# Expert weights streamed through a mixture-of-experts stage: down products one matrix later, a held first load, a last pass in pairs of rows

## The chip, the cores and the metric

The kernel runs on one core of one Trainium2 chip. The metric is the device time of one execution in microseconds (us), the median of several runs; lower is better. All data is fp32.

## The reference

One encoder block on 2048 tokens of 1024 features: two groups of attention heads, an output projection, a mixture of experts, and a last RMSNorm. The change lies in the last two:

```python
gate = g_w * jax.nn.softmax(top_val, axis=-1)     # top group, then the top 2 of its 8 experts
def run_block(args):                              # xb: rows of tokens sent to expert e
    xb, e = args
    h = jax.nn.silu(xb @ w_gate[e]) * (xb @ w_up[e])
    return h @ w_down[e]
y = jnp.zeros((N, D), x.dtype).at[slot_tok].add(ys * slot_gate[:, None])
...
h = h + hier_moe(rms_norm(h, norm2_gain[l]), ...)
return rms_norm(h, final_gain)
```

There are 64 experts; w_gate and w_up are 1024 x 512 each, w_down is 512 x 1024: 6 MiB of weights per expert, 384 MiB in all.

## The kernel before, in words

Up to about 1676 us the kernel computes attention, the projection and the routing; they are not touched. Then comes the **experts' stage**, to about 2951 us, and **the last pass** (`finish`) to the end.

**Pieces.** Each of an expert's three matrices is loaded from DRAM in two pieces of 1 MiB (`raw`, 128 partitions x 8 KB), 384 pieces in all; `halves_of` lists them in order. All loads (L1370) are issued by SP, in that order, each into one of 9 places (`NAHEAD` 5 + `NB` 4). The first five are issued before the stage ("ahead"). Below, piece 5 is the sixth one, and piece 383 the last. DRAM reads and writes of all queues go through the same 16 DMA engines.

**Split.** For exactness, each piece is split into a high part `wh` (a cast, ACT, L1498) and a low part `wl = raw - wh` (a subtraction, DVE, L1500), with `WN` places each. TensorE (PE) multiplies with both: 24 products of 512 columns for each matrix, `pg` (gate) and `pu` (up) at L1547, `py` (down) at L1553.

**An expert's way.** POOL gathers its 100 rows from `d_xn` into `xg` by an indirect DMA (L1507). PE transposes them (L1520), and ACT and DVE split them into `xT` (L1525, L1527). After the gate products ACT takes silu (L1568), and after the up products DVE multiplies into `hh` (L1571). PE transposes `hh` (L1577), and ACT and DVE split it into `hT` (L1581, L1583). After the down products ACT scales them into `o` (L1590), and POOL adds `o` to rows of `d_h` by an indirect DMA, the "put" (L1595). The last put waits for the seven before it, and the last pass reads `d_h` after the last put.

**What sets the order.** The helper functions of `experts` (`loads`, `weights`, `inputs`, `products`, `silu`, `sums`) are generators that ask a planner (`Plan.run`) for an engine with `ask(engine, us, ..., take=places, urge)`. The planner simulates all engines with these costs, and the order in which it grants the requests becomes the program order of PE, ACT, DVE and POOL. On the chip each engine then runs its instructions in that order and waits at each for what it needs. The loads' order on SP is that of `halves_of` whatever the costs.

**The last pass** loads `d_h` in 8 transfers of 1 MiB (L1625; 4 KB pieces per partition), and for each of 16 blocks of 128 rows takes the sum of squares (ACT, L1632), two small POOL operations (L1633, L1634), the scaling (DVE, L1635) and a store of 512 KB (L1636). A second call of `experts` for overflowing rows exists in the program and is not executed with these inputs.

Of the kernel before, what the change touches and what calls it, by code (L numbers as in the profile page):

```python
# [8 lines left out]
F32 = mybir.dt.float32  # L9
# [3 lines left out]
AF = mybir.ActivationFunctionType  # L13
OP = mybir.AluOpType
AX = mybir.AxisListType

P = 128
T = 2048
NT = T // P
D = 1024  # L20
KD = D // P
EPS = 1e-6
# [6 lines left out]
NG = 8  # L29
NE = 64  # L30
CAP = 100
# [13 lines left out]
NPL = 3  # L45
NAHEAD = 5
NB = 4
WN = 4
PYN = 2
WLAND = 30  # L50
LF = 2.9
# [69 lines left out]
class Plan:  # L121
# [19 lines left out]
    def give(self, token, *names):  # L141
        for n in names:
            self.slots.setdefault(n, []).append(token)
# [34 lines left out]
def ask(eng, dur, *deps, take=(), due=None, urge=0.0):  # L178
    return eng, dur, deps, take, due, urge
# [7 lines left out]
def halves_of(n):  # L187


    seq = [(0, 0, 0), (0, 0, 1)]  # L190
    for e in range(n):
        seq += [(e, 1, 0), (e, 1, 1)] + [(e + 1, 0, 0), (e + 1, 0, 1)] * (e + 1 < n) + [(e, 2, 0), (e, 2, 1)]
    return seq


# [1 line left out]
def hybrid_encoder_kernel(ctx, tc, x, norm1_gain, w_in, gla_up_fwd, gla_up_fwd_bias, gla_up_bwd,  # L197
# [3 lines left out]
    nc = tc.nc  # L201
# [65 lines left out]
    def rms_scale(dst, ss, n):  # L267

        nc.vector.tensor_scalar(dst, ss, 1.0 / n, EPS, op0=OP.mult, op1=OP.add)
        nc.gpsimd.tensor_tensor(dst, dst, mhalf[0:dst.shape[0], :dst.shape[-1]], op=OP.pow)  # L270
# [539 lines left out]
    with ExitStack() as ph:  # L810
# [555 lines left out]
        def load_expert(e, raw, which, half):  # L1366
            w = (w_gate, w_up, w_down)[which]

            v = w[0, e].rearrange("(p k) n -> p (k n)", p=P)
            nc.sync.dma_start(raw, v[:, half * 2048:(half + 1) * 2048])  # L1370

        listed = []
        last_h, raw_pools, ahead, taken = [], [], [], [0]

        def next_raw(load):
            pool = raw_pools[len(raw_pools) > 1 and taken[0] % (NAHEAD + NB) >= NAHEAD]
            taken[0] += 1
            raw = pool.tile([P, 2048], F32, name="raw")
            load(raw)
            return raw  # L1380

        def load_ahead(t):
# [28 lines left out]
    with ExitStack() as ph:  # L1411
# [5 lines left out]
        xgs = [wp.tile([CAP, D], F32, name=f"xg{j}") for j in range(2)]  # L1417
        for t in xgs:
            nc.gpsimd.memset(t, 0.0)

        start = wp.tile([P, NE], F32, name="start")
        bexp = wp.tile([1, OBLK], I32, name="bexp")
# [40 lines left out]
        def experts(blocks, ahead=(), then=None):  # L1463


            plan = Plan({"xg": 2, "xT": 2, "hT": 2, "wh": WN, "wl": WN, "pt": 2, "pg": 1, "pu": 1, "py": PYN,
                         "hh": 2, "o": 2, "visit": NG, "raw": NAHEAD + NB - len(ahead)})
            add, give = plan.add, plan.give
            raws, ws, xTs, hTs, ps, nb = {}, {}, {}, {}, {}, len(blocks)
            puts = {}  # L1470
            data_dep = mybir.DependencyInfo(mybir.DependencyClass.Sync, mybir.DependencyReason.DATA)
            seq = halves_of(nb)
            listed_at = TL if ahead else 0.0, "dma"
# [5 lines left out]
            def loads():  # L1479
                for n, (e, which, half) in enumerate(seq):  # L1480
                    t = (0.0, "dma")
                    if n < len(ahead):
                        raws[n] = ahead[n]
                    else:
                        t = yield ask("dma", 2.91, take=("raw",))
                        raws[n] = next_raw(lambda raw: blocks[e][1](raw, which, half))
                    give((t[0] + 2.0, "dma"), f"raw{n}")

            def weights(n):

                k = 4 if seq[n][1] < 2 else 2
                t = yield ask("act", 1.9, take=(f"raw{n}", "wh"))
                if n + 1 < len(seq):
                    add(weights(n + 1))
                raw = raws.pop(n).rearrange("p (k n) -> p k n", k=k)
                wh = sp.tile([P, k, 2048 // k], F32R, name="wh", bufs=WN)
                wl = sp.tile([P, k, 2048 // k], F32R, name="wl", bufs=WN)
                nc.scalar.copy(wh, raw)  # L1498
                t = yield ask("dve", 2.28, t, take=("wl",))
                nc.vector.tensor_tensor(wl, raw, wh.bitcast(F32), op=OP.subtract)  # L1500
                ws[n] = wh, wl
                give(t, "raw", f"w{n}")

            def inputs(e):
                xg = xgs[e % 2]
                t = yield ask("pool", 1.95, listed_at, take=("xg",), urge=20.0)
                nc.gpsimd.indirect_dma_start(  # L1507
                    out=xg, out_offset=None, in_=d_xn, in_offset=bass.IndirectOffsetOnAxis(ap=column(e, 0), axis=0),
                    bounds_check=T - 1, oob_is_err=False)
                t = yield ask("dma", 1.18, (t[0] + 1.5, "pool"), urge=20.0)  # L1510
                if e + 1 < nb:
                    add(inputs(e + 1))
                tx = t[0] + 1.8, "dma"
                xT = sp.tile([P, 2, KD, CAP], F32R, name="xT")
                xk = xg.rearrange("c (p k) -> c k p", k=KD)
                for b in range(2):
                    t = yield ask("pe", 0.42, tx, take=("pt",) if b else ("pt", "xT"), urge=20.0)
                    pt = pp.tile([P, 4, CAP], F32, name="pt")
                    for k in range(4):
                        nc.tensor.transpose(pt[:, k, :], xk[:, 4 * b + k], ident[0:CAP, 0:CAP])  # L1520
                    if b:
                        give(t, "xg")
                    bs = slice(4 * b, 4 * b + 4)
                    t = yield ask("act", 0.49, t, urge=20.0)
                    nc.scalar.copy(xT[:, 0, bs], pt)  # L1525
                    t = yield ask("dve", 0.57, t, urge=20.0)
                    nc.vector.tensor_tensor(xT[:, 1, bs], pt, xT[:, 0, bs].bitcast(F32), op=OP.subtract)  # L1527
                    give(t, "pt")
                xTs[e] = xT
                give(t, f"xT{e}")  # L1530

# [55 lines left out]
            def sums(e):  # L1587
                t = yield ask("act", 1.25, take=(f"py{e}", "o"), urge=40.0)
                o = sp.tile([CAP, D], F32, name="o")
                nc.scalar.activation(o, ps.pop((e, 2)).rearrange("p a b -> p (a b)"), AF.Identity, scale=column(e, 1))  # L1590
                give(t, "py")
                if e + 1 < nb:
                    add(sums(e + 1))
                t = yield ask("pool", 2.9, t, take=("visit",), urge=40.0)
                put = nc.gpsimd.indirect_dma_start(  # L1595
                    out=d_h, out_offset=bass.IndirectOffsetOnAxis(ap=column(e, 0), axis=0), in_=o, in_offset=None,
                    bounds_check=T - 1, oob_is_err=False, compute_op=OP.add)
                for p in range(max(e - NG + 1, 0), e):
                    if e + 1 < nb:
                        tc.declare_no_dep(put.ins, puts[p].ins, reason="tokens of other groups")  # L1600
                    else:
                        tc.add_manual_dep(put.ins, puts[p].ins.name, data_dep, reason="all rows are done")
                if e >= NG:
                    tc.add_manual_dep(put.ins, puts[e - NG].ins.name, data_dep, reason="the group's expert before")
                puts[e] = put
                t = yield ask("dma", 1.18, (t[0] + 1.5, "pool"), urge=40.0)
                give((t[0] + 2.0, "dma"), "visit", "o")
                if then and e == nb // 2:
                    add(then(plan))
# [12 lines left out]

        def finish():

            hs = [next_raw(lambda raw, i=i: nc.sync.dma_start(  # L1625
                raw.rearrange("p (a d) -> p a d", a=2), d_h[2 * i * P:2 * (i + 1) * P].rearrange("(a p) d -> p a d", p=P)))
                for i in range(NT // 2)]
            for i in range(NT):
                h = hs[i // 2][:, i % 2 * D:(i % 2 + 1) * D]
                ss = sp.tile([P, 1], F32, name="ss", bufs=4)  # L1630
                sq = pp.tile([P, 2, 512], F32, name="py", bufs=PYN)
                nc.scalar.activation(sq.rearrange("p a b -> p (a b)"), h, AF.Square, accum_out=ss)  # L1632
                nc.gpsimd.tensor_scalar(ss, ss, 1.0 / D, EPS, op0=OP.mult, op1=OP.add)  # L1633
                nc.gpsimd.tensor_tensor(ss, ss, mhalf[:, :1], op=OP.pow)  # L1634
                nc.vector.scalar_tensor_tensor(h, h, ss, gf, op0=OP.mult, op1=OP.mult)  # L1635
                nc.sync.dma_start(out2[i * P:(i + 1) * P], h)  # L1636
        finish()

        nblk_v = nc.values_load(nblk, min_val=0, max_val=OBLK)
        with tc.If(nblk_v > 0):  # L1640
# [19 lines left out]
            with tc.For_i(0, nblk_v, 1) as b:  # L1660
# [5 lines left out]
                def load(raw, which, half):  # L1666
                    w = (w_gate, w_up, w_down)[which]
                    v = w[0, bass.ds(e, 1)].rearrange("o (p k) n -> p (o k n)", p=P)
                    nc.sync.dma_start(raw, v[:, half * 2048:(half + 1) * 2048])
# [33 lines left out]
```

## Time and profile before

| | |
|---|---|
| median of 3 runs | 2999.57 us (2995.89 to 3000.0) |
| profiled execution | 2999.41 us |
| span of its instructions | 2997.4 us (2.0 us lie outside the span) |
| mean granted TensorE clock | 0.977 |
| PE busy | 94% of the span |
| DMA moved | 647.0 MB, mean 216 GB/s over the span |

The span runs from the first to the last instruction on the core; a clock of 1.0 stands for TensorE's full speed. PE's 94% is an average over stages; the experts' stage is 42% of the time, and what bounds it has to be read there. All times below are us from the span's start.

### The profile page before, as it was taken

What the parts mean: (1) busy time and instruction counts of PE and PEld (TensorE: products, weight loads), DVE (VectorE), ACT (ScalarE), POOL (GpSimd) and SP (SyncE); (2) the same over time, 40 slices, a digit from 0 to 9 for tenths busy, and PEclk for the clock granted to TensorE, in tenths of its full rate; (3) what the DMA queues carried; (4) which work ended last, traced back from release to release, by engine and by line L of the source; (5) the groups of instructions that cost most, each with busy time, mean ns of one, the idle gap of its engine ahead of it and who ended that gap; (6) DMA issues with size and microseconds to landing.
All of it is one profiled execution on the core that took longest, in us unless ns stands there. A gap on an engine that the chain in (4) does not pass through costs nothing.

```text
span 2997.4 us, 38671 instructions
## 1 busy us (share of the span) xinstructions
PE 2819.4 (94%) x13776; PEld 2096.9 (70%) x13776; DVE 2222.5 (74%) x3214; ACT 1857.9 (62%) x2776; POOL 468.2 (16%) x349
## 2 busy tenths in 40 slices
PE   7999999999999999999999699999999999999992
PEld 6888788887677777777677466666666666666661
DVE  6654788888666766776766688887778878788784
ACT  4433333333676777777776477777777767777773
POOL 3443111111000000000000211111111111112114
PEclk9999999999899999999999799999999999999996
DMA  7874333223522222221221799999999999999996
GB/s 256 293 263 167 140 105 108 76 104 124 195 66 66 68 67 67 66 71 60 75 64 57 284 357 356 356 357 345 347 346 351 342 346 355 347 349 346 342 317 233
DMA packets 177316, 647.00 MB, mean 216 GB/s; under 512 B 39013, under 2 KB 53703, under 8 KB 123549
## 3 DMA queue, kind: packets, MB, share of 16 engines
q1 hardware_dynamic: 138942, 590.92, 55.1%
q0 software_dynamic: 23712, 34.36, 5.2%
q10 hardware_dynamic: 14464, 19.21, 2.0%
q8 instruction: 109, 1.79, 0.3%
q14 instruction: 89, 0.73, 0.1%
HBM read 546.08 MB, written 117.13 MB: 221 GB/s over the span
## 4 chain that ended last, share of the span: by engine, by line
PE 72%; DMA 14%; DVE 5%; ACT 5%; issue 2%; POOL 1%; SPq 0%; ACTq 0%; POOLq 0%; DVEq 0%
PE py L1553 9%; DMA raw<-in_w_up_dram 8%; PE pu L1547 7%; PE pg L1547 7%; PE pm L1007 6%; PE pm L681 4%; PE pa L1356 4%; PE ps L1328 4%; PE pa L1354 4%; PE pa L1355 4%; PE ps L1329 4%; DMA raw<-in_w_down_dram 3%; PE pv L334 3%; PE pqk L334 3%; DVE wl L1500 2%
## 5 line engine op out<-in xcount | busy, mean ns | idle before, releaser
L1500 DVE TENSOR_TENSOR wl<-raw,wh 128x2048 fp32r<-128x2048 f32 x384 | 872.3, 2289 | 242.8 <-ACT wh L1498 242.2
L1498 ACT CAST wh<-raw 128x2048 fp32r<-128x2048 f32 x384 | 726.0, 1903 | 245.9 <-PE py L1553 102.0
L1343 DVE TENSOR_TENSOR p_l<-p,p_h 128x512 fp32r<-128x512 f32 x512 | 344.0, 689 | 200.2 <-ACT p_h L1340 194.1
L1332 ACT ACTIVATE p<-ps 128x512 f32<-128x512 f32 x512 | 296.4, 599 | 150.3 <-PE ps L1329 132.6
L1553 PE MATMUL py<-wh,hT 128*100 128x512 f32 x1024 | 306.5, 412 | 56.2 <-ACT hT L1581 42.5
L683 DVE TENSOR_REDUCE nm<-pm 128x1 f32<-128x1024 f32 x256 | 305.0, 1216 | 46.7 <-PE pm L681 46.6
L1547 PE MATMUL pg<-wh,xT 128*100 128x512 f32 x1024 | 334.7, 397 | 0.0
L1547 PE MATMUL pu<-wh,xT 128*100 128x512 f32 x1024 | 330.5, 393 | 0.0
L1340 ACT CAST p_h<-p 128x512 fp32r<-128x512 f32 x448 | 268.9, 624 | 5.8
L1553 PEld LDWEIGHTS py<-wh,hT 128*100 128x100 f32 x1024 | 163.0, 169 | 143.2 <-ACT hT L1581 52.7
L1547 PEld LDWEIGHTS pg<-wh,xT 128*100 128x100 f32 x1024 | 170.5, 167 | 64.1
L1547 PEld LDWEIGHTS pu<-wh,xT 128*100 128x100 f32 x1024 | 168.0, 164 | 67.5
L1507 POOL DMA_INDIRECT xg<-d_xn,L x64 | 124.9, 1952 | 577.5 <-PE pt L1520 570.2
L1328 PE MATMUL ps<-q,K 128*128 128x512 f32 x512 | 210.6, 411 | 1.2 <-ACT p L1332 0.8
L1354 PE MATMUL pa<-p_h,V 128*66 128x512 f32 x512 | 204.4, 399 | 0.0
L1356 PE MATMUL pa<-p_l,V 128*66 128x512 f32 x512 | 202.7, 396 | 0.9 <-DVE p_l L1343 0.9
L1329 PE MATMUL ps<-q,K 65*128 65x512 f32 x512 | 203.4, 397 | 0.0
L1547 PE MATMUL pg<-wl,xT 128*100 128x512 f32 x512 | 202.0, 395 | 0.0
L1355 PE MATMUL pa<-p_h,V 128*64 128x512 f32 x512 | 201.5, 393 | 0.0
L1547 PE MATMUL pu<-wl,xT 128*100 128x512 f32 x512 | 200.5, 392 | 0.0
L1595 POOL DMA_INDIRECT d_h<-o,L x64 | 102.1, 1595 | 471.6 <-ACT o L1590 471.6
L681 PE MATMUL pm<-K,q 128*128 128x512 f32 x512 | 169.6, 416 | 1.1 <-DVE nm L683 1.1
(416 smaller groups left out, 5098.9 us busy)
## 6 DMA issues: line engine op xcount, KB each, us to landing
raw<-in_w_gate_dram SPq DMA_DIRECT2D x128, 1024.0 KB
raw<-in_w_up_dram SPq DMA_DIRECT2D x128, 1024.0 KB
raw<-in_w_down_dram SPq DMA_DIRECT2D x128, 1024.0 KB
d_uT<-uT SPq DMA_DIRECT2D x16, 1024.0 KB
uT<-d_uT SPq DMA_DIRECT2D x15, 1024.0 KB
x_t<-in_x_dram SPq DMA_DIRECT2D x16, 512.0 KB
wraw<-in_w_in_dram SPq DMA_DIRECT2D x32, 256.0 KB
d_q<-q ACTq DMA_DIRECT2D x16, 512.0 KB
```

The source lines that it names most:

```text
L683: nc.vector.tensor_reduce(nm[:, h, b:b + 1], pm, axis=AX.XY, op=OP.max, negate=True)
L1328: nc.tensor.matmul(ps, lhsT=K1[:, kv, ks], rhs=r1, start=True, stop=False)
L1329: nc.tensor.matmul(ps, lhsT=K2[:, kv, ks], rhs=r2, start=False, stop=True)
L1332: nc.scalar.activation(p, ps, AF.Exp)
L1343: nc.vector.tensor_tensor(p_l, p, p_h.bitcast(F32), op=OP.subtract)
L1354: nc.tensor.matmul(pa, lhsT=hi, rhs=p_h, start=(kt == 0), stop=False)
L1355: nc.tensor.matmul(pa[0:DH], lhsT=V[:, kt, kv, 0:DH], rhs=p_h, start=False, stop=False)
L1356: nc.tensor.matmul(pa, lhsT=hi, rhs=p_l, start=False, stop=(kt == NT - 1))
L1498: nc.scalar.copy(wh, raw)
L1500: nc.vector.tensor_tensor(wl, raw, wh.bitcast(F32), op=OP.subtract)
L1547: nc.tensor.matmul(acc_p, lhsT=xTs[e][:, a, k, :], rhs=w[:, kk, :], start=(k == 0 and a == 0 and w is wh), stop=(k == KD - 1 and a == 1))
L1553: nc.tensor.matmul(acc_p[:, c], lhsT=hTs[e][:, a, k, :], rhs=w[:, kk, c * 512:(c + 1) * 512], start=(k == 0 and a == 0 and w is wh), stop= ...
```

## The change

Four things are changed. (1) `halves_of`: the order of pieces was gate 0; then for each expert e up e, gate e+1, down e. It is now gate e, up e, down e-1, so that a gate and an up matrix stand between an expert's up products and its down products (one matrix, the next gate, stood there before). `WN` goes from 4 to 5. (2) Piece 5 waits until expert 0's gather has landed, and the first subtraction waits until POOL has issued that gather (a 1x1 memset, `issued`, stands behind it on POOL); both of expert 0's transposes are asked for ahead of its splits, with a higher urge. (3) Costs of the planner: a load 2.91 to 2.6, a gather 1.18 to 0.8, a put 1.18 to 1.3. (4) `finish` takes two adjacent rows of tokens to a partition: 8 loads and 8 stores of 1 MiB, 8 KB for each partition, and `rms_scale` for a pair (one DVE and one POOL operation) in place of two POOL operations per block.

```diff
-WN = 4
+WN = 5
...
-    seq = [(0, 0, 0), (0, 0, 1)]
-    for e in range(n):
-        seq += [(e, 1, 0), (e, 1, 1)] + [(e + 1, 0, 0), (e + 1, 0, 1)] * (e + 1 < n) + [(e, 2, 0), (e, 2, 1)]
+    seq = []
+    for e in range(n + 1):
+        seq += [(x, which, half) for x, which in ((e, 0), (e, 1), (e - 1, 2)) for half in range(2) if 0 <= x < n]
...
-        def next_raw(load):
+        def next_raw(load, after=None):
...
+            ld = load(raw)
+            if after is not None:
+                tc.add_manual_dep(ld.ins, after.ins.name, ..., reason="the first rows go before")
...
-                        t = yield ask("dma", 2.91, take=("raw",))
+                        after = ahead and n == len(ahead)
+                        t = yield ask("dma", 2.6, take=("raw", "landed") if after else ("raw",))
...
-                t = yield ask("dve", 2.28, t, take=("wl",))
+                t = yield ask("dve", 2.28, t, take=("wl",) if n else ("wl", "issued"))
...
+                if e == 0:
+                    first.extend((get, nc.gpsimd.memset(issued, 0.0)))
+                    give(t, "issued")
-                t = yield ask("dma", 1.18, (t[0] + 1.5, "pool"), urge=20.0)
+                t = yield ask("dma", 0.8, (t[0] + 1.5, "pool"), urge=20.0)
...
-                t = yield ask("dma", 1.18, (t[0] + 1.5, "pool"), urge=40.0)
+                t = yield ask("dma", 1.3, (t[0] + 1.5, "pool"), urge=40.0)
...
+            pair = lambda a, i: a[2 * i * P:2 * (i + 1) * P].rearrange("(p a) d -> p (a d)", a=2)
+            hs = [next_raw(lambda raw, i=i: nc.sync.dma_start(raw, pair(d_h, i))) for i in range(NT // 2)]
+            for i, h in enumerate(hs):
+                ss = sp.tile([P, 2], F32, name="ss", bufs=4)
+                for a in range(2):
...
+                rms_scale(ss, ss, D)
+                for a in range(2):
+                    ha = h[:, a * D:(a + 1) * D]
+                    nc.vector.scalar_tensor_tensor(ha, ha, ss[:, a:a + 1], gf, op0=OP.mult, op1=OP.mult)
+                nc.sync.dma_start(pair(out2, i), h)
```

Three places show what the planner makes of it. Line numbers move: L1547 becomes L1569, L1553 becomes L1575, L1577 becomes L1599, L1500 becomes L1505, L1527 becomes L1548, L1571 becomes L1593 and L1507 becomes L1514.

**Middle of the stage, PE, before.** The last gate products of one expert, transposes of the next expert's rows and of this expert's `hh`, and the first down products (numbers tell tiles apart):

```order
L1547 MATMUL pg_22468<-wl_22433,xT_22103 100x512
L1547 MATMUL pg_22468<-wh_22432,xT_22103 100x512
L1520 MATMUL pt_22504<-cst_sb_99,xg1_18103 128x100 x4
L1577 MATMUL pt_22512<-cst_sb_99,hh_22365 128x100 x4
L1553 MATMUL py_22530<-wh_22446,hT_22517 100x512 x2
```

The same place on PE in the changed kernel:

```order
L1569 MATMUL pu_22382<-wh_22309,xT_21941 100x512
L1540 MATMUL pt_22420<-cst_sb_99,xg1_18103 128x100 x4
L1575 MATMUL py_22430<-wh_22351,hT_22308 100x512 x2
L1575 MATMUL py_22430<-wl_22352,hT_22308 100x512 x2
L1575 MATMUL py_22430<-wh_22351,hT_22308 100x512 x4
L1575 MATMUL py_22430<-wl_22352,hT_22308 100x512 x2
L1575 MATMUL py_22430<-wh_22351,hT_22308 100x512 x2
L1599 MATMUL pt_22448<-cst_sb_99,hh_22386 128x100 x4
L1575 MATMUL py_22430<-wh_22366,hT_22308 100x512 x2
```

Before, the down products follow right behind the transposes that make their own `hT` (22517). Now they use the `hT` of the expert before (22308), and the transposes of `hh` (22386), for a later `hT`, stand between the two halves of the down products.

**Start of the stage, POOL and DVE, changed kernel.** POOL's first gathers, and DVE from the last step of the routing list (L1306) on:

```order
L1514 DMA xg0_18102<-d_xn_90,L_67 100x1024
L1518 MEMSET issued_18106 1x1
L1514 DMA xg1_18103<-d_xn_90,L_67 100x1024
```

```order
L1306 TENSOR_TENSOR L_67<-pt_18078,L_67 100x64
L1505 TENSOR_TENSOR wl_18119<-raw_17808,wh_18118 128x2048
L1505 TENSOR_TENSOR wl_18126<-raw_17837,wh_18125 128x2048
L1548 TENSOR_TENSOR xT_18121<-pt_18134,xT_18121 128x400
L1548 TENSOR_TENSOR xT_18121<-pt_18141,xT_18121 128x400
L1505 TENSOR_TENSOR wl_18131<-raw_17888,wh_18130 128x2048
```

Before, POOL's row of the memset was not there, and DVE had three subtractions in a row behind L1306; now two, the first of which waits for POOL's memset. On SP the load of piece 5 has one more wait, for the gather's landing, and all later loads stand behind it.

**End of the stage, PE, changed kernel.** The last down products of the last but one expert (`py_27338`) and of the last (`py_27372`):

```order
L1575 MATMUL py_27338<-wh_27277,hT_27246 100x512 x2
L1599 MATMUL pt_27352<-cst_sb_99,hh_27306 128x100 x4
L1575 MATMUL py_27338<-wh_27289,hT_27246 100x512 x2
...
L1575 MATMUL py_27338<-wh_27289,hT_27246 100x512 x2
L1575 MATMUL py_27372<-wh_27312,hT_27357 100x512 x2
```

DVE's end in the changed kernel:

```order
L1505 TENSOR_TENSOR wl_27278<-raw_27125,wh_27277 128x2048
L1505 TENSOR_TENSOR wl_27290<-raw_27147,wh_27289 128x2048
L1505 TENSOR_TENSOR wl_27313<-raw_27170,wh_27312 128x2048
L1505 TENSOR_TENSOR wl_27326<-raw_27201,wh_27325 128x2048
L1593 TENSOR_TENSOR hh_27306<-pu_27302,hh_27306 100x512
L1605 TENSOR_TENSOR hT_27357<-pt_27352,hT_27357 128x400
```

Both kernels have the last expert's multiply (`hh`) behind the last piece's subtraction on DVE. Before, the last expert's up products stood behind the down products of the last but one; now its transposes stand in the middle of those, and between the two last experts' down products there is nothing else.

## Rows read from the trace of the kernel before

**Rows 1.** Page, busy time by engine and costliest groups (busy us, mean ns | idle before)

```profile
PE 2819.4 (94%) x13776; PEld 2096.9 (70%) x13776; DVE 2222.5 (74%) x3214; ACT 1857.9 (62%) x2776; POOL 468.2 (16%) x349
...
L1500 DVE TENSOR_TENSOR wl<-raw,wh 128x2048 fp32r<-128x2048 f32 x384 | 872.3, 2289 | 242.8 <-ACT wh L1498 242.2
L1498 ACT CAST wh<-raw 128x2048 fp32r<-128x2048 f32 x384 | 726.0, 1903 | 245.9 <-PE py L1553 102.0
```

**Rows 2.** Windows mid-stage: length, busy of PE, PEld, DVE, ACT, POOL, clock, DMA share, GB/s

```profile
1800.00:1900.00 100.00, 97.09 (x448) 70.06 (x447) 81.96 (x53) 74.81 (x59) 18.23 (x11) 1.00 1.02 356
2500.00:2600.00 100.00, 93.87 (x430) 67.43 (x429) 79.82 (x51) 71.50 (x57) 17.15 (x10) 1.00 1.01 350
```

**Rows 3.** Chain of waits around one expert's down products: start, us, what

```profile
1980.53 0.60 ACT hh L1568
...
1981.51 0.42 ACT hT L1581
1981.97 5.90 PE py L1553 x24
```

**Rows 4.** Windows of the casts (L1498) alone, cast to cast: length, ACT, clock, share, GB/s

```profile
2020.20:2887.30 867.10, 499.71 (x264) 0.99 1.00 347
```

**Rows 5.** Windows at the start of the stage, columns as in Rows 2

```profile
1668.00:1680.00 12.00, 2.39 (x9) 1.76 (x8) 9.38 (x33) 7.99 (x8) 4.97 (x5) 0.59 0.93 342
1680.00:1687.00 7.00, 0.00 (x0) 0.00 (x0) 2.92 (x2) 0.00 (x0) 5.05 (x2) 0.50 1.02 428
1687.00:1694.00 7.00, 0.31 (x2) 0.31 (x3) 0.00 (x0) 0.00 (x0) 0.00 (x0) 0.50 0.76 238
1694.00:1700.00 6.00, 4.83 (x21) 3.64 (x20) 3.81 (x5) 1.97 (x4) 2.44 (x2) 0.50 0.11 21
1700.00:1709.00 9.00, 9.00 (x39) 6.37 (x38) 3.79 (x4) 6.60 (x5) 0.47 (x1) 0.95 0.70 208
1709.00:1720.00 11.00, 10.80 (x54) 7.88 (x53) 10.12 (x9) 8.19 (x8) 1.23 (x1) 1.00 0.94 346
```

**Rows 6.** Windows at the end of the weights, columns as in Rows 2

```profile
2920.00:2926.00 6.00, 5.38 (x25) 3.77 (x24) 5.13 (x4) 4.69 (x4) 0.00 (x0) 1.00 0.13 40
2926.00:2930.00 4.00, 4.00 (x19) 2.86 (x18) 3.02 (x2) 2.00 (x2) 0.00 (x0) 1.00 0.00 0
```

**Rows 7.** Timeline of POOL, gathers at the start: start, us, what [idle before]

```profile
1677.12 6.86 POOL L1507 DMA_INDIRECT xg<-d_xn,L  x1 [7.03 <-DVE L L1306]
...
1697.18 1.06 POOL L1507 DMA_INDIRECT xg<-d_xn,L  x1 [11.83 <-PE pt L1520]
```

**Rows 8.** Timeline of DVE and of PE over the same stretch

```profile
1676.24 6.68 DVE L1500 TENSOR_TENSOR wl<-raw,wh 128x2048 fp32r<-128x2048 f32 x3
...
1693.69 0.93 PE L1520 MATMUL pt<-cst_sb,xg 100*128 100x100 f32 x4 [17.77 <-DMA xg<-d_xn,L]
```

**Rows 9.** The gathers' line, all 64, us from issue to landing

```profile
DMA to landing us min/median/max: 5.3/11.7/16.5
```

**Rows 10.** Chain of waits, the end of the stage

```profile
2935.44 0.70 DVE hh L1571
...
2936.18 0.74 PE pt L1577 x4
2936.94 0.50 ACT hT L1581
...
2937.49 5.78 PE py L1553 x24
2943.29 1.12 ACT o L1590
...
2944.70 6.63 DMA d_h<-o,L
```

**Rows 11.** Timeline of POOL, the last put but one

```profile
2931.32 1.58 POOL L1595 DMA_INDIRECT d_h<-o,L  x1 [16.39 <-ACT o L1590]
```

**Rows 12.** Windows of the last pass, columns as in Rows 2

```profile
2954.00:2992.00 38.00, 0.00 (x0) 0.00 (x0) 20.55 (x16) 18.05 (x32) 28.18 (x32) 0.50 1.03 415
```

More of the change, by code (lines that the diff above doesn't have):

```diff
@@ L1369, in load_expert @@
             v = w[0, e].rearrange("(p k) n -> p (k n)", p=P)
-            nc.sync.dma_start(raw, v[:, half * 2048:(half + 1) * 2048])
+            return nc.sync.dma_start(raw, v[:, half * 2048:(half + 1) * 2048])
         listed = []
         last_h, raw_pools, ahead, taken = [], [], [], [0]
-        def next_raw(load):
+        def next_raw(load, after=None):
             pool = raw_pools[len(raw_pools) > 1 and taken[0] % (NAHEAD + NB) >= NAHEAD]
@@ L1378, in next_raw @@
             raw = pool.tile([P, 2048], F32, name="raw")
-            load(raw)
+            ld = load(raw)
+            if after is not None:
+                tc.add_manual_dep(ld.ins, after.ins.name, mybir.DependencyInfo(
+                    mybir.DependencyClass.Sync, mybir.DependencyReason.DATA), reason="the first rows go before")
             return raw
@@ L1419, in hybrid_encoder_kernel @@
             nc.gpsimd.memset(t, 0.0)
+        issued = wp.tile([1, 1], F32, name="issued")
         start = wp.tile([P, NE], F32, name="start")
@@ L1466, in experts @@
             plan = Plan({"xg": 2, "xT": 2, "hT": 2, "wh": WN, "wl": WN, "pt": 2, "pg": 1, "pu": 1, "py": PYN,
-                         "hh": 2, "o": 2, "visit": NG, "raw": NAHEAD + NB - len(ahead)})
+                         "hh": 2, "o": 2, "visit": NG, "raw": NAHEAD + NB - len(ahead), "issued": 0, "landed": 0})
             add, give = plan.add, plan.give
             raws, ws, xTs, hTs, ps, nb = {}, {}, {}, {}, {}, len(blocks)
-            puts = {}
+            puts, first = {}, []
             data_dep = mybir.DependencyInfo(mybir.DependencyClass.Sync, mybir.DependencyReason.DATA)
@@ L1484, in loads @@
                     else:
-                        t = yield ask("dma", 2.91, take=("raw",))
-                        raws[n] = next_raw(lambda raw: blocks[e][1](raw, which, half))
+                        after = ahead and n == len(ahead)
+                        t = yield ask("dma", 2.6, take=("raw", "landed") if after else ("raw",))
+                        raws[n] = next_raw(lambda raw: blocks[e][1](raw, which, half), first[0] if after else None)
                     give((t[0] + 2.0, "dma"), f"raw{n}")
@@ L1498, in weights @@
                 nc.scalar.copy(wh, raw)
-                t = yield ask("dve", 2.28, t, take=("wl",))
-                nc.vector.tensor_tensor(wl, raw, wh.bitcast(F32), op=OP.subtract)
+                t = yield ask("dve", 2.28, t, take=("wl",) if n else ("wl", "issued"))
+                lo = nc.vector.tensor_tensor(wl, raw, wh.bitcast(F32), op=OP.subtract)
+                if n == 0:
+                    tc.add_manual_dep(lo.ins, first[1].ins.name, data_dep, reason="the first rows go before")
                 ws[n] = wh, wl
@@ L1506, in inputs @@
                 t = yield ask("pool", 1.95, listed_at, take=("xg",), urge=20.0)
-                nc.gpsimd.indirect_dma_start(
+                get = nc.gpsimd.indirect_dma_start(
                     out=xg, out_offset=None, in_=d_xn, in_offset=bass.IndirectOffsetOnAxis(ap=column(e, 0), axis=0),
                     bounds_check=T - 1, oob_is_err=False)
-                t = yield ask("dma", 1.18, (t[0] + 1.5, "pool"), urge=20.0)
+                if e == 0:
+                    first.extend((get, nc.gpsimd.memset(issued, 0.0)))
+                    give(t, "issued")
+                t = yield ask("dma", 0.8, (t[0] + 1.5, "pool"), urge=20.0)
                 if e + 1 < nb:
@@ L1513, in inputs @@
                 tx = t[0] + 1.8, "dma"
+                if e == 0:
+                    give(tx, "landed")
                 xT = sp.tile([P, 2, KD, CAP], F32R, name="xT")
                 xk = xg.rearrange("c (p k) -> c k p", k=KD)
[L1516 to L1522, printed above, removed]
-                    bs = slice(4 * b, 4 * b + 4)
[L1524 to L1528, printed above, removed]
+                steps = [("pe", 0), ("act", 0), ("dve", 0), ("pe", 1), ("act", 1), ("dve", 1)]
+                urge, ts, pts = 20.0, {}, {}
+                if e == 0:
+                    steps.sort(key=lambda x: ("pe", "act", "dve").index(x[0]))
+                    urge = 60.0
+                for eng, b in steps:
+                    bs = slice(4 * b, 4 * b + 4)
+                    if eng == "pe":
+                        t = yield ask("pe", 0.42, tx, take=("pt",) if b else ("pt", "xT"), urge=urge)
+                        pts[b] = pp.tile([P, 4, CAP], F32, name="pt")
+                        for k in range(4):
+                            nc.tensor.transpose(pts[b][:, k, :], xk[:, 4 * b + k], ident[0:CAP, 0:CAP])
+                        if b:
+                            give(t, "xg")
+                    elif eng == "act":
+                        t = yield ask("act", 0.49, ts[b], urge=urge)
+                        nc.scalar.copy(xT[:, 0, bs], pts[b])
+                    else:
+                        t = yield ask("dve", 0.57, ts[b], urge=urge)
+                        nc.vector.tensor_tensor(xT[:, 1, bs], pts[b], xT[:, 0, bs].bitcast(F32), op=OP.subtract)
+                        give(t, "pt")
+                    ts[b] = t
                 xTs[e] = xT
@@ L1623, in finish @@
         def finish():
[L1625 to L1636, printed above, removed]
+            pair = lambda a, i: a[2 * i * P:2 * (i + 1) * P].rearrange("(p a) d -> p (a d)", a=2)
[3 more added lines that the diff above has]
+                for a in range(2):
+                    sq = pp.tile([P, 2, 512], F32, name="py", bufs=PYN)
+                    nc.scalar.activation(sq.rearrange("p a b -> p (a b)"), h[:, a * D:(a + 1) * D], AF.Square,
+                                         accum_out=ss[:, a:a + 1])
+                rms_scale(ss, ss, D)
[3 more added lines that the diff above has]
+                nc.sync.dma_start(pair(out2, i), h)
         finish()
```

## The prediction

> **What bounds the kernel now.** I read the page first, then windows of 100 us through the experts' stage, then the chain of waits at its middle and its end, then timelines of the queues where the change cuts. The page shows PE busy for 94% of the span [rows 1], which tempts one to look for PE's idle time. The windows [rows 2] are to be read from their last columns: PE is busy 97 of 100 us in one and 94 in another, but the share of the DMA engines is 1.01 to 1.02 in both, at 356 and 350 GB/s. The chain of waits there runs through PE: silu (0.60 us) and the split of hT (0.42) pass through ACT one after the other, with a split of the next rows between, and 1.44 us after silu began the down products run [rows 3]. This is a stall of PE, but is it what sets the stage's pace?
>
> The casts give the pace. From the start of one at 2020.20 to the start of another at 2887.30 there are 264 of them in 867.1 us, 3.284 us for each, with the DMA share at 1.00 [rows 4]: loads were never out of work. With loads alone on the queues they run at 428 GB/s (from 1680 to 1687, [rows 5]), which is 2.45 us for a piece of 1.0486 MB. So an expert takes 6 x 3.284 = 19.70 us, its six pieces alone would take 14.70, and the 5.0 us between are what one gather and one put cost the loads. At the end of the weights one sees where: from 2920 to 2926 the DMA share is 0.13, two engines of 16, at 40 GB/s, and then nothing [rows 6]. Two engines bring the last pieces long after the other 14 are done. I conclude that the stage is bound by its two slowest DMA engines, with PE close behind: it idles 6.1 us in 100 [rows 2], 1.2 us per expert.
>
> **1. Order of pieces and a fifth place.** The change moves the down products away from the transposes that they wait for. With PE as the bound it would return most of 1.2 us per expert. But pieces, gathers and puts are the same in number and size, so by the DMA reading the pace stays at 3.284 us and PE waits as much for weights as it waited for hT: 0 in the middle of the stage. Bounds: the two windows [rows 2] differ by 1.7% in rate, about 20 us over the some 1,200 us of loading. As much as that could go either way if gathers and puts fall differently among the loads; a gain of 1.2 us x 62 experts = 74 us is the naive extreme.
>
> **2. The start.** The first gather takes POOL 6.86 us, from 1677.12 to 1683.98 [rows 7], while DVE does three subtractions without a gap from 1676.24 to 1682.92 [rows 8]. A gather that meets no such row takes 1.06 us [rows 7]: the first one ends 1.06 us after the subtractions, as if it had only begun then. PE's wait for it ends at 1693.69 [rows 8]. Now the first subtraction waits for the gather, so I take it at 1.06 us, and its landing at the shortest time seen, 5.3 us from issue [rows 9], since no load is on the queues: 1677.1 + 5.3 = 1682.4. What waits behind: on DVE two subtractions and then the splits, some 1 us later than before; on SP all loads from piece 5 on, which go at 1682.5 instead of from 1669 on, with first bytes an assumed 1.2 us later, at 1683.7.
>
> What this costs is a matter of bytes. Before, from 1668 to 1720, the windows [rows 5] add up to 4.10 + 3.00 + 1.67 + 0.13 + 1.87 + 3.81 = 14.57 MB; there was a hole from 1694 to 1709, while the places were full and PE waited for rows. After: 36.3 us x 0.428 = 15.54 MB from 1683.7 on. Off this go three gathers; two of them brought the rate to 238 for 7 us, (428 - 238) x 7 / 2 = 0.67 MB each, so 13.5 MB; and what still moves before 1683.7 (rows of d_xn, the last gain, the first gather) I estimate at 1.3 MB. That makes 14.8, ahead by 0.2 MB or 0.5 us. Counted by share of engines, before stood idle for 12 x 0.07 + 7 x 0.24 + 6 x 0.89 + 9 x 0.30 + 11 x 0.06 = 11.2 us, and after would for 12.6: 1.4 us later. With gathers that cost only their bytes (100 rows of 4 KB, 0.41 MB) it is 0.8 MB more, 2.4 us earlier. I take the middle of the two ends, **-0.5**, with bounds -2.4 and +1.4.
>
> **3. The end.** Let the last piece land at 2926 [rows 6]. Before, one more expert's up products stood behind down products, and the chain ended in hh, transposes, hT and the last down products (0.70, 0.74, 0.50, 5.78 us), PE being done at 2943.27; then o, and the put that landed at 2944.70 + 6.63 = 2951.33 [rows 10], 25.3 us after the piece. After: the last piece is cast (1.90) and subtracted (2.29) [rows 1], and only then comes the last expert's multiply (0.70), for which PE's transposes stand in the middle of the next to last down products: 2926 + 0.1 + 1.90 + 2.29 + 0.70 = 2931.0. Then transposes 0.74, the second half of one down product (5.78 / 2 = 2.9) and the whole last one (5.78): PE ends at 2940.4, 2.9 us earlier. But a new wait comes up: the last put waits for the put before. That was 13.4 us ahead (2931.32 [rows 11] against 2944.70), and is now only a down product ahead: its o begins at 2934.6, it is issued 1.4 us later (as 2943.29 to 2944.70) at 2936.0, and lands 6.63 later at 2942.7. The last put could go at 2940.4 + 1.4 = 2941.8; it goes at about 2942.8 and lands at 2949.4. The end comes **-1.9** us after the last piece, with bounds -2.9 (no such wait) and +3.2 (the put before takes the 11.7 us of a gather among loads [rows 9]).
>
> **4. The last pass.** From 2954 to 2992 the DMA share is 1.03 at 415 GB/s; DVE is busy 21 of these 38 us, ACT 18, POOL 28 [rows 12]. It moves 15.8 MB. Pieces of 8 KB at the loads' 428 GB/s would take 36.85 us, a gain of 1.15. Part of the traffic is now stores, for which 428 is not shown, so I take **-0.9** (bounds -1.15 and 0). Fewer POOL and DVE steps save nothing, since DMA covers them; were that cover gone, the pairs would show as gaps between stores.
>
> The Trainium skill, "DMA: Bandwidth & Descriptors", section "Why small descriptors are slow", gives each packet some 3 cycles of overhead at 32 bytes a cycle. By that, 8 KB instead of 4 KB would save 1.1% of the last pass, an estimate of 0.4 us, and the sum would be 2996.6. The rows' difference in rate, 3%, is larger, and decides.
>
> **5. Planner costs** only change the order, which is the one weighed above: 0.
>
> The sum: -0.5 - 1.9 - 0.9 = -3.3 us, from 2999.41 of the profiled execution (0.2 us under the median): **2996.1**.
>
> **Rivals.**
> - *Nothing gained* (2998 to 3001): the held loads cost their bound of +1.4, and the put before lands 2 us later than alone, so that the end's -1.9 goes: +1.4 + 0 - 0.9 = +0.5, 2999.9. It decides from 8.6 us for that put on; alone on the queues it has no reason for it.
> - *Held for a slow gather (slower)*: if the gather still lands at about 1693.7 [rows 8], because its 6.86 us were not the subtractions', loads go 11.3 us later: -0.5 + 11.3 - 1.9 - 0.9 = +8, 3007. It decides from a landing at about 1689 on. For it speaks that no row shows a gather beside fewer subtractions; against it, the match of 1.06 us.
> - *PE is the bound*: 62 experts x 1.2 = -74, about 2925. Against it speak shares of 1.00 and equal spacing of pieces; for it, only the chain through PE.
> - *The slow engines are relieved*: gathers and puts fall into other gaps and cost 5% less, 0.25 x 61 = -15, near 2981; the rate's differences between windows [rows 2] allow as much.
>
> On the second rival the Trainium skill, "SBUF — State Buffer", is of two minds: its section "Who interferes with whom" says that a DVE operation with both inputs in SBUF holds up a GpSimd one that reads SBUF, but it infers that such a subtraction does not hold back the writing of descriptors. By the inference the gather would stay slow and the time near 3007; the trace agrees with the first (the 1.06 us above).
>
> **How the numbers follow.** The sum holds with 0.57 (its own range 2990 to 2999.5; a third of this below 2993.6), nothing gained 0.11, slow gather 0.08, PE-bound 0.06, relieved engines 0.18. A measurement tells 0.2%, 6.0 us, from no change: faster means under 2993.6, slower over 3005.6. Faster: 0.19 + 0.06 + 0.18 = 0.43; same: 0.38 + 0.11 = 0.49; slower 0.08. The range of 2979 to 3001 leaves out the slow gather, PE-bound, and a third of the relieved case, 0.20.
>
> **What would show it.** Right: the first gather at about 1.1 us on POOL and landing near 1682, no hole in DMA between 1694 and 1709, casts still 3.28 us apart with a DMA share of 1.00 while the down products no longer wait for hT, a last put that waits for the one before, 425 GB/s or more in the last pass. Wrong: a spacing of casts under 3.25 us (engines relieved or PE the bound), or a first gather over 5 us.

## The result and the profile after

The changed kernel takes 2982.57 us (median of 6 runs, 2978.75 to 2986.49) against 2999.26 us for the kernel before (6 runs): ratio 0.9947, 95% interval 0.9933 to 0.9961. It is 16.7 us faster; 3.3 were forecast. The profiled execution took 2981.33 us with a span of 2979.4, 18.0 less than before.

Where these 18.0 us lie follows from when pieces land (the semaphore updates that each load sends, in the trace). Counted from the routing list's end (L1306, 1676.3 us before, 1677.5 after; this 1.2 us lies ahead of everything that the change touches):

| | before | after | difference |
|---|---|---|---|
| list's end to piece 15 landed | 43.8 | 46.9 | +3.1 |
| piece 15 to piece 383 landed | 1206.1 | 1183.0 | -23.1 |
| piece 383 to the first load of d_h | 25.2 | 25.7 | +0.5 |
| that load to the span's end | 46.1 | 46.3 | +0.2 |

So the middle of the stage brought all of the gain and more: 368 pieces at 3.215 us in place of 3.277 us.

The windows at the start, columns as in [rows 2], answer to [rows 5]:

```profile
1668.00:1680.00 12.00, 3.35 (x19) 2.56 (x19) 6.11 (x34) 6.45 (x8) 4.76 (x7) 0.63 0.24 88
1680.00:1687.00 7.00, 1.60 (x8) 1.29 (x8) 5.68 (x5) 2.01 (x3) 3.93 (x2) 0.50 0.54 156
1687.00:1694.00 7.00, 6.55 (x25) 4.91 (x26) 6.75 (x4) 4.34 (x4) 0.58 (x1) 0.67 1.02 343
1694.00:1700.00 6.00, 6.00 (x28) 4.28 (x27) 4.00 (x3) 5.97 (x6) 0.83 (x1) 1.00 1.03 330
1700.00:1709.00 9.00, 9.00 (x47) 6.84 (x46) 6.84 (x6) 5.38 (x6) 0.43 (x1) 1.00 1.02 356
1709.00:1720.00 11.00, 11.00 (x53) 8.10 (x52) 10.88 (x8) 7.27 (x7) 2.87 (x2) 1.00 1.02 343
```

The hole of before (share 0.11 from 1694 to 1700) is gone, but a new one stands from 1668 to 1683, and behind it the rate is 330 to 356 GB/s, not 428. The timelines of POOL (first gather), DVE (first subtractions) and SP (piece 5) show the order that was wanted: gather, then subtractions, then loads:

```profile
1678.32 1.19 POOL L1514 DMA_INDIRECT xg<-d_xn,L  x1 [7.03 <-DVE L L1306]
...
1679.63 4.49 DVE L1505 TENSOR_TENSOR wl<-raw,wh 128x2048 fp32r<-128x2048 f32 x2 [2.10 <-POOL issued L1518]
...
1683.82 0.33 SPq L1370 DMA_DIRECT2D raw<-in_w_gate_dram  x1
```

In the middle, the casts from one start to another, as in [rows 4]; then, from 2000 to 2850 us, waits of PE and ACT before (in each row who waited for what: us in total, times, longest), and the longest waits of DVE, ACT and PE after:

```profile
2021.01:2859.12 838.11, 490.49 (x260) 0.98 0.99 353
```

```profile
PE py L1553 <- ACT hT L1581: 31.4, 42, 2.2
...
ACT wh L1498 <- DMA raw<-in_w_up_dram: 30.6, 33, 2.5
...
ACT wh L1498 <- DMA raw<-in_w_down_dram: 28.1, 30, 2.0
```

```profile
DVE wl L1505 <- ACT wh L1503: 155.3, 154, 2.6
ACT wh L1503 <- DMA raw<-in_w_up_dram: 98.7, 60, 3.4
ACT wh L1503 <- DMA raw<-in_w_gate_dram: 49.0, 36, 2.4
PEld pt L1599 <- DVE hh L1593: 37.5, 14, 3.8
```

260 casts in 838.11 us are 3.224 us for each, where [rows 4] gave 3.284. The down products no longer wait for hT; ACT waits longer for loads instead (148 us in these two rows, 59 before). The DMA share is 0.99, where it was 1.00, but the rate is 353 GB/s and not 347: with their share as full as before, the engines carry the same bytes in less time.

The end, in the chain of waits (start, us, what), answers to [rows 10], and the window of the last pass to [rows 12]:

```profile
2918.64 6.76 DMA d_h<-o,L
...
2926.32 6.72 DMA d_h<-o,L
...
2933.10 4.88 DMA raw<-d_h
```

```profile
2936.00:2974.00 38.00, 0.00 (x0) 0.00 (x0) 20.56 (x24) 17.50 (x32) 5.59 (x8) 0.50 1.01 417
```

The last put waits for the one before it, and only then come the loads of d_h; the last pass runs at 417 GB/s against 415.

### The profile page after: what moved, and what is told of

Same layout as the page of the kernel before. It is cut to its first block, busy times and chain, and to the rows that moved or that the text cites. A ratio compares the mean times of both kernels' runs of the same rounds, so it can differ in the third digit from the quotient of the medians.

```text
span 2979.4 us, 38648 instructions
## 1 busy us (share of the span) xinstructions
PE 2812.6 (94%) x13776; PEld 2101.0 (71%) x13776; DVE 2225.4 (75%) x3222; ACT 1852.0 (62%) x2776; POOL 448.4 (15%) x326
## 4 chain that ended last, share of the span: by engine, by line
PE 59%; DMA 21%; issue 7%; DVE 6%; ACT 5%; POOL 1%; ACTq 0%; SPq 0%; POOLq 0%; DVEq 0%
DMA raw<-in_w_gate_dram 10%; DMA raw<-in_w_up_dram 7%; PE pm L1007 6%; PE pm L681 4%; PE pa L1356 4%; PE ps L1328 4%; PE pa L1354 4%; PE pa L1355 4%; PE py L1575 4%; PE pg L1569 4%; PE ps L1329 4%; PE pv L334 3%; PE pqk L334 3%; DVE wl L1505 2%; ACT wh L1503 2%
## 5 line engine op out<-in xcount | busy, mean ns | idle before, releaser
L1505 DVE TENSOR_TENSOR wl<-raw,wh 128x2048 fp32r<-128x2048 f32 x384 | 873.5, 2289 | 218.2 <-ACT wh L1503 215.6
L1569 PE MATMUL pg<-wh,xT 128*100 128x512 f32 x1024 | 335.4, 398 | 0.0
L1569 PE MATMUL pu<-wh,xT 128*100 128x512 f32 x1024 | 330.7, 394 | 0.0
L1575 PE MATMUL py<-wh,hT 128*100 128x512 f32 x1024 | 320.7, 416 | 0.0
L1514 POOL DMA_INDIRECT xg<-d_xn,L x64 | 109.2, 1707 | 914.6 <-PE pt L1540 904.5
L1569 PEld LDWEIGHTS pu<-wh,xT 128*100 128x100 f32 x1024 | 168.1, 164 | 68.2
L1569 PEld LDWEIGHTS pg<-wh,xT 128*100 128x100 f32 x1024 | 170.7, 167 | 64.6
L1575 PEld LDWEIGHTS py<-wh,hT 128*100 128x100 f32 x1024 | 170.3, 176 | 55.6
L1569 PE MATMUL pg<-wl,xT 128*100 128x512 f32 x512 | 202.0, 395 | 0.0
L1569 PE MATMUL pu<-wl,xT 128*100 128x512 f32 x512 | 200.5, 392 | 0.0
L1575 PE MATMUL py<-wl,hT 128*100 128x512 f32 x512 | 166.3, 407 | 0.0
```

The costliest lines, as they stand in the source:

```text
L1505: lo = nc.vector.tensor_tensor(wl, raw, wh.bitcast(F32), op=OP.subtract)
L1569: nc.tensor.matmul(acc_p, lhsT=xTs[e][:, a, k, :], rhs=w[:, kk, :], start=(k == 0 and a == 0 and w is wh), stop=(k == KD - 1 and a == 1))
L1575: nc.tensor.matmul(acc_p[:, c], lhsT=hTs[e][:, a, k, :], rhs=w[:, kk, c * 512:(c + 1) * 512], start=(k == 0 and a == 0 and w is wh), stop= ...
```

## The experiments

**Two theories for the faster middle.** Look at POOL's timeline before, from 2513 us, and after, from 2515 us:

```profile
2513.53 1.73 POOL L1507 DMA_INDIRECT xg<-d_xn,L  x1 [9.16 <-PE pt L1520]
2521.66 1.59 POOL L1595 DMA_INDIRECT d_h<-o,L  x1 [6.39 <-ACT o L1590]
```

```profile
2515.84 2.12 POOL L1514 DMA_INDIRECT xg<-d_xn,L  x1 [17.55 <-PE pt L1540]
2518.26 3.56 POOL L1617 DMA_INDIRECT d_h<-o,L  x1 [0.30 <-ACT wh L1503]
```

Before, a put started 8.1 us behind a gather. In the new order of pieces the second half of the transposes that free a gather's place stands right behind the end of the down products on PE (2514.86 and 2513.12 us here), and the put starts 2.4 us behind the gather. Theory N: gather and put close together cost the loads less than the same two apart. Theory S: the gain comes from PE's earlier start, the fifth place or the later down products, and the distance is an accident.

**1. Puts apart again, all else as changed** (`a_putlate`). Each put waits for the first half of the up products two experts on.

```diff
+                    if (which, half) == (1, 0) and e >= 2:
+                        late[e - 2] = lastmm[0]
+                        give(t, f"late{e - 2}")
...
+                if held:
+                    tc.add_manual_dep(put.ins, late[e].ins.name, data_dep, reason="put later")
```

> The changed kernel, with each put held back until the first half of the up products two experts on has run, so that it starts some 8 us behind the gather in place of some 2 us; nothing else is changed. Theory N (gather and put issued close together cost the loads less than the same two apart): the spacing of casts goes from 3.245 back to about 3.28 us, the time to about 2994 (+8 to +14 us on the changed kernel's 2982.6), ratio to before about 0.998. Theory S (the faster loads come of PE's earlier start, the fifth place and the later down products, not of the puts): no change, 2982 to 2984, ratio 0.995.

Measured: 3002.1 us, ratio to before 1.0012 (1.0003 to 1.0021); the whole gain is gone, more than the 8 to 14 us expected. POOL shows the distance, 8.9 us:

```profile
2507.41 1.29 POOL L1515 DMA_INDIRECT xg<-d_xn,L  x1 [6.43 <-PE pt L1541]
2516.28 2.60 POOL L1624 DMA_INDIRECT d_h<-o,L  x1 [7.59 <-issue]
```

**2. Puts close by, all else as before** (`b_putlate`): the same edit in the kernel before, with (0, 1), the gate products, in place of (1, 0).

> The kernel before, with each put held back until the gate products two experts on have run, so that it starts within some 2 us of a gather in place of 8 to 10 us behind it; nothing else is changed. Theory N: the spacing of casts goes from 3.282 to about 3.25 us and the time falls by 8 to 14 us, to about 2988, ratio 0.996. Theory S: no change, 2997 to 3001, ratio 1.000.

Measured: 2959.28 us, ratio 0.986 (0.9845 to 0.9875): 39.9 us faster than before with none of the change in it, some three times what Theory N expected, and 23 faster than the changed kernel. The put now starts 2.4 us ahead of the next gather:

```profile
2510.62 2.13 POOL L1602 DMA_INDIRECT d_h<-o,L  x1 [15.35 <-ACT hh L1574]
2513.06 1.10 POOL L1508 DMA_INDIRECT xg<-d_xn,L  x1 [0.30 <-issue]
```

Loads no longer set the pace in this run. Its window from 2000 to 2600 us (columns as in [rows 2]) and waits of ACT and PE from 2000 to 2850 us:

```profile
2000.00:2600.00 600.00, 582.25 (x2679) 419.64 (x2678) 496.74 (x327) 446.06 (x350) 106.30 (x64) 1.00 1.01 361
```

```profile
ACT wh L1499 <- PE py L1556: 62.2, 45, 1.4
...
PE py L1556 <- ACT hT L1587: 25.1, 43, 0.6
```

No cast waits for a load here: ACT waits until PE frees places, and PE, busy for 824.7 of these 850 us, waits for hT alone in nearly all the rest. So PE with its wait for hT is the bound, at 18.97 us per expert, and the DMA share stands at 1.01 all the same.

**3. The old order of pieces, the rest as changed** (`a_oldorder`): `halves_of` as it was.

> The changed kernel with the order of pieces of before (gate of the next expert between up and down); the fifth place, the held first load, the costs and the last pass stay as changed. Theory N: put and gather are apart again, the spacing goes back to about 3.28 us, time about 2994 to 2998, ratio 0.998 to 1.000. Theory S with the start and the fifth place as the cause: most of the gain stays, 2984 to 2988, ratio about 0.9955.

Measured: 3002.34 us, ratio 1.0011 (1.0002 to 1.0020), put 8.1 us behind the gather. The fifth place, the held load, the costs and the last pass together gain nothing.

**4. Four places** (`a_wn4`): `WN = 5` to `WN = 4`.

> The changed kernel with four places for split weights in place of five. Theory N: no change in the spacing of casts (3.245 us), time 2982 to 2985, ratio 0.995. Theory S with the fifth place as the cause: spacing near 3.28 us, time 2992 to 2998, ratio 0.998 to 1.000.

Measured: 2977.01 us, ratio 0.9918 (0.9904 to 0.9932). The fifth place does not bring the gain. That four places are 5.6 us faster is not shown to be their doing: of the 4.0 us between the two profiled executions, all 4.0 lie in an earlier end of the routing list, ahead of everything that the run changes. This end lies between 1672.0 and 1677.5 us in the profiled executions of all the runs, so a few us between two runs need not come from the stage. Theory S falls in all its forms with these four.

**5. What a gather and a put cost.** Three runs leave out the low part of the weights (`wl`), its subtraction and a third of PE's products (`d_light`); two of these leave out 48 puts or 52 gathers as well. They are for measuring alone, and each was executed once.

```diff
-                            for a, w in ((0, wh), (0, wl), (1, wh)):
+                            for a, w in ((0, wh), (1, wh)):
...
-                nc.vector.tensor_tensor(wl, raw, wh.bitcast(F32), op=OP.subtract)
```

> The changed kernel without the low part of the weights: no subtraction on DVE and no products with wl, a third of PE's products left out; all transfers stay. If the two slowest DMA engines set the pace: spacing of casts 3.24 us as in the changed kernel. If PE does: 2.9 us or less (PE's work falls from 17.9 to about 12 us per expert, ACT's is about 14).

> As the run without low parts, and the 48 puts of experts 8 to 55 are left out too. If gather and put share the 5 us about evenly: spacing 2.45 + 2.5 / 6 = 2.87 us in that stretch. If the put is the dear one (it reads and writes d_h): near 2.6 us; if the gather is: near 3.1 us.

> As the run without low parts, and the gathers of experts 8 to 59 are left out (their rows are those of earlier experts), the puts stay. Evenly shared: 2.87 us. Put dear: near 3.1 us; gather dear: near 2.6 us. If the two prices add up to more than the 4.7 us that gather and put close together cost, nearness saves the difference.

The windows from 2000 to 2600 us (columns as in [rows 2]) of the changed kernel, the light one, without puts and without gathers:

```profile
2000.00:2600.00 600.00, 574.22 (x2624) 417.58 (x2623) 488.14 (x321) 433.01 (x342) 107.70 (x62) 0.98 1.00 354
```

```profile
2000.00:2600.00 600.00, 440.15 (x1823) 319.32 (x1822) 71.25 (x130) 423.13 (x334) 81.80 (x61) 0.84 1.00 345
```

```profile
2000.00:2600.00 600.00, 482.86 (x2035) 350.16 (x2034) 79.52 (x144) 473.35 (x372) 36.22 (x34) 0.88 1.01 370
```

```profile
2000.00:2600.00 600.00, 495.51 (x2135) 360.38 (x2134) 84.14 (x152) 487.32 (x389) 55.32 (x35) 0.90 1.01 390
```

With PE busy for only 440 of 600 us and DVE for 71, the DMA share is still 1.00 and the pace no better: transfers set it, as the prediction read. It is even slower, 3.313 us per piece, and gather and put have drifted 8.9 us apart. Prices by landings of pieces 100 to 300, as 6 x (spacing - 2.45), 2.45 us being a piece at 428 GB/s:

| run | put starts, from the nearest gather (median) | spacing, us | us per expert |
|---|---|---|---|
| before | 8.1 behind | 3.290 | 5.0 |
| `a_oldorder` | 8.1 behind | 3.280 | 5.0 |
| `a_putlate` | 8.9 behind | 3.285 | 5.0 |
| `d_light` | 8.9 ahead | 3.313 | 5.2 |
| changed kernel | 2.2 behind | 3.228 | 4.7 |
| `a_wn4` | 2.2 behind | 3.240 | 4.7 |
| `c_putfirst` | 2.4 ahead | 3.228 | 4.7 |
| `e_best` | 2.0 ahead | 3.197 | 4.5 |
| `b_putlate` (PE is the bound) | 2.4 ahead | 3.162 | at most 4.3 |
| gathers alone (`d_light_noput`) | | 2.963 | 3.1 |
| puts alone (`d_light_noget`) | | 2.815 | 2.2 |

A gather alone costs 3.1 us and a put alone 2.2, together 5.3. Apart they cost 5.0 to 5.2, nearly that sum; close together 4.5 to 4.7, and at most 4.3 in run 2, whose pace is PE's. Of the forms expected, "put dear" is out; the spacings lie between "evenly shared" and "gather dear". A put that is held also moves against the loads and the products, so no single run changes the distance alone; but both orders of pieces give 3.28 to 3.29 us with the two apart, and every run with the two close gives 3.24 or less.

**6. Put first, then gather** (`c_putfirst`): the gather is placed behind its neighbouring put on POOL.

```diff
-                t = yield ask("pool", 1.95, listed_at, take=("xg",), urge=20.0)
+                t = yield ask("pool", 1.95, listed_at, take=("xg", f"put{e - 5}") if 8 <= e < nb else ("xg",), urge=20.0)
...
+                give(t, f"put{e}")
```

> The changed kernel, with each gather placed behind its neighbouring put on POOL, so that the put goes first and the gather follows some 2 us later, as in the run of before with held puts, where the spacing of casts was 3.18 us. If the order within the pair matters: spacing 3.18 in place of 3.24 us, time near 2964 (370 x 0.05 = 19 us less). If only nearness matters: spacing 3.24, time 2980 to 2985.

Measured: 2973.87 us, ratio 0.9921 (0.9908 to 0.9935), but a spacing of 3.228 us as in the changed kernel. The order within the pair alone does not explain run 2's 3.162. The profiled execution's span is 7.5 us shorter than the changed kernel's: 4.5 lie in the list's earlier end and 4.3 between the list and the last piece, and 1.3 of these are lost behind it.

**7. Without the hold** (`a_nohold`): piece 5 and the first subtraction wait for no gather.

```diff
-                        after = ahead and n == len(ahead)
+                        after = False
...
-                t = yield ask("dve", 2.28, t, take=("wl",) if n else ("wl", "issued"))
+                t = yield ask("dve", 2.28, t, take=("wl",))
```

> The changed kernel without the held first load: piece 5 does not wait for the first gather and the first subtraction does not wait for POOL; order, places, costs and last pass as changed. By the prediction's step 2 (the hold is worth -0.5 us, bounds -2.4 to +1.4): time 2981 to 2985, piece 15 landing within 2 us of the changed kernel's, counted from the routing list's end. If the hold costs what the trace of the changed kernel seems to show (piece 15 lands 3.1 us later than before, counted so): 2979 to 2980. If the hold pays through PE's earlier start: 2988 or more.

Measured: 2974.86 us, ratio 0.9915 (0.9901 to 0.9928), 7.7 us less than the changed kernel and below all three times expected. Its windows at the start:

```profile
1668.00:1680.00 12.00, 2.86 (x14) 2.07 (x12) 8.56 (x33) 8.25 (x9) 4.97 (x5) 0.64 0.91 337
1680.00:1687.00 7.00, 0.00 (x0) 0.00 (x0) 3.80 (x2) 0.00 (x0) 2.33 (x3) 0.50 1.03 385
1687.00:1694.00 7.00, 1.60 (x8) 1.29 (x8) 1.41 (x3) 1.85 (x3) 1.06 (x1) 0.50 0.97 288
1694.00:1700.00 6.00, 2.57 (x9) 2.02 (x10) 3.04 (x3) 1.43 (x2) 0.00 (x0) 0.50 0.83 223
```

Loads flow from 1669 on, and piece 15 lands 39.1 us after the list, not 46.9, though PE begins later. Of the 7.8 us, 2.2 are left at the last piece of the two profiled executions. The hold costs time; how much is less certain (run 9).

**8, 9, 10. All together.** `e_best` has four places, puts held until the next expert's down products are done (so 2.0 us ahead of a gather), and a last put that does not wait for the put before it; the last pass waits for both. `f_best` takes the hold away as well, `f_best5` has five places again.

> The changed kernel with four places, each put held until the down products of the next expert are done, so that it starts some 2.5 us ahead of a gather, and a last put that does not wait for the put before it (the last pass waits for both). Theory N, put first: spacing 3.17 to 3.19 us in place of 3.24 (-18 us), end of the stage 2 us nearer to the last piece: time 2952 to 2960. If the put's place ahead of the gather gave its gain only in the old order of pieces: spacing 3.22 to 3.25, time 2968 to 2976.

> The run with held puts, four places and a last put without a wait (2959.4 us), and the held first load taken away too. If the two gains add: 2959.4 - 7.7 = 2951.7 us, piece 15 some 7 us earlier and the last piece 3 to 7 us earlier. If the stage gives the earlier start back (as most of the 7.8 us at piece 15 were given back by the last piece in the run without the hold): 2956 to 2960.

> The same with five places for split weights. If the fifth place matters only at the end (four places brought the end of the stage 3.3 us nearer to the last piece): 2 to 4 us more than with four. If it feeds the stage (spacing 3.236 against 3.248 us): 2 to 4 us less.

Measured: 2959.39, 2958.02 and 2956.23 us; ratios 0.9868 (0.9853 to 0.9883), 0.9869 (0.9853 to 0.9886) and 0.986 (0.9843 to 0.9876). These do not differ from one another or from run 2 by what the intervals can tell. Taking the hold away, worth 7.7 us in run 7, brings 1.4 us here, so the gains did not add to 2951.7 as one of the expectations had it; the fifth place, 5.6 us slower in run 4, is 1.8 us faster here. The best of them is 42 us under the kernel before and 26 under the changed one. POOL in `e_best`:

```profile
2518.07 1.97 POOL L1624 DMA_INDIRECT d_h<-o,L  x1 [11.28 <-issue]
2520.35 1.90 POOL L1517 DMA_INDIRECT xg<-d_xn,L  x1 [0.30 <-issue]
```

And the end in `f_best5`, in the chain of waits: PE ends at 2901.9, and the last put goes 1.4 us later, where it went 3.6 us later in the changed kernel (2922.7 to 2926.32). PE itself ends later behind the last piece, so that from there to the first load of d_h it is 25.6 us in `f_best5` and 25.7 in the changed kernel:

```profile
2901.96 1.10 ACT o L1616
2903.06 0.28 issue
2903.35 6.64 DMA d_h<-o,L
```

## Why the prediction was right in its range and wrong in its size

The time lies in the stated range, but not by the sum: 2982.57 is below the sum's own range (2990 to 2999.5), which had 0.57. It is in the stated range because that range took in a rival with a chance of 0.18. The prediction's own sign of being wrong came up too: a spacing of casts under 3.25 us, with 3.224 measured. The misses of steps 2 to 4, +7.1 us together, hid a third of the -23.1 us that step 1 had at 0.

- **What bounds the stage** was right for these two kernels. The light run removed a third of PE's products and nearly all of DVE's work without a gain, and in `a_putlate` the down products' wait for hT is gone as well, at 3.285 us per piece. The rival "PE is the bound" falls for them; run 2 reaches that bound. The share, from which the prediction read it, does not tell the two apart: it is 1.01 in run 2 too. The landings do. Each load sends 16 updates; over pieces 100 to 300 the 14th, 15th and 16th of them come 12.0, 21.7 and 23.1 us after the load's issue in the kernel before (medians), 19.9, 21.8 and 23.4 us in the changed kernel, and 9.3, 11.4 and 15.7 us in `b_putlate`. So in the kernel before two parts of a load lag some 10 us behind the rest, as two slow engines would make them; in run 2 the last three lag far less.
- **Step 1** is the one that failed, in size: "0 in the middle of the stage". It measured -23.1 us between pieces 15 and 383. The step counted gathers and puts and held their price fixed because their number and size are; it gave the possibility that they "fall differently among the loads" as a bound of 20 us and took 0. The order of pieces moved the put from 8.1 to 2.2 us behind the gather, which takes 0.3 to 0.4 us off 5.0 per expert (x 61 = about 20). This is the rival "slow engines are relieved" (forecast 2981, chance 0.18). That the transposes that free `xg` and the end of the down products meet could have been read from PE's order, of which the rows shown ahead of the prediction end too soon.
- **Step 2** was right in its parts and wrong in its sum. The first gather took 1.19 us and landed 5.5 us after its issue (1.06 and 5.3 forecast), and piece 5 went 6.3 us after the list's end, as worked out; its first bytes came 1.0 us later (1.2 assumed). But -0.5 became +3.1, outside the bounds. The 13.5 MB put down for the time from 1683.7 on assumed 428 GB/s less three gathers; measured were 332 GB/s in these 36.3 us, 12.1 MB. In all, the windows from 1668 to 1720 moved 13.5 MB in place of the 14.8 forecast and the 14.57 of before. Run 7 shows that the hold is no gain. The rival "held for a slow gather" did not happen.
- **Step 3** named the new wait and priced it too low: -1.9 became +0.5. The put before landed 6.76 us after its issue (6.63 forecast), but the last put went 0.9 us after that landing, not 0.1, and the last piece's cast began 1.1 us after landing, not 0.1; PE finished 15.3 us after the last piece (14.4 forecast).
- **Step 4**: -0.9 became +0.2. 417 against 415 GB/s: at 8 KB pieces the mix of loads and stores does not reach the loads' own 428. The estimate of 0.4 us, worked out in the prediction from the Trainium skill, "DMA: Bandwidth & Descriptors", section "Why small descriptors are slow", is too little to be told in these rows: 2 GB/s of 415 are 0.2 us of the 38.

What stays open is why two bursts near one another cost less on the DMA engines than two apart, and why with the put ahead of the gather the loads keep up with 3.162 us per piece in the old order of pieces, but hold ACT up at 3.197 and 3.228 in the new one. The records of the packets do not say which engine they ran on, so the slow engines could not be followed one by one.

## What to carry to other kernels

Where a stream of loads fills the DMA engines, look at when other transfers fall into it, and not only at their number: bring the small indirect ones together, and check on their queue's timeline that they are. A change of order on the computing engines can move them by accident; hold one of them back, alone, to see what their distance is worth before crediting the reorder. Read what sets the pace from who waits for a load, not from the share of the DMA engines. A load stream that is held back for a latency pays with its own bytes, unless the engines would have been idle.

## What the runs showed of the hardware

A gather of 100 rows of 4 KB (0.41 MB, 0.96 us at 428 GB/s) costs a full stream of loads 3.1 us, and an adding put of the same size 2.2 us, by one execution each. The two cost 5.0 to 5.2 us per expert when 8 to 9 us lie between their starts, and 4.5 to 4.7 us at 2 us (at most 4.3 in run 2). With the share of the engines at 0.99 to 1.01 in all these cases and rates from 345 to 390 GB/s, a full share does not say that the rate can't rise, nor, by run 2, that anything waits for a load.
